# Sample states read a second time in turned layout in place of TensorE transposes, and two mask tiles moved to a short-lived pool

## The chip, the core and the metric

The kernel runs on one core of one Trainium2 chip. The metric is the device time of one launch in microseconds. The core has a matrix engine (TensorE, "PE" in the profile, with its weight loads listed as "PEld"), three elementwise engines (VectorE "DVE", ScalarE "ACT", GpSimd "POOL") and a queue engine (SyncE "SP") that here does nothing but issue DMA transfers. Each engine works through its own list of instructions strictly in order. An instruction that has to wait for another engine or for a transfer also holds everything behind it on its own engine.

## What is computed

One inference step of a two-layer decoder, for a prompt of 1024 tokens and for 8 samples of 8 tokens each. Layer 0 is a Mamba-2 state-space (SSD) mixer, layer 1 is latent attention. Only layer 0 is touched here. Cut to what matters:

```python
def ssd_mixer(h, conv_buf, ssm_state, w_in, ...):
    proj = jnp.einsum('btd,de->bte', h, w_in)          # z | x, B, C | dt
    xbc = silu(causal_conv(xbc, conv_buf, conv_w, conv_b))
    dt = softplus(dt_raw + dt_bias); a_head = -exp(a_log)
    y, new_state = ssd_scan(xs, dt, a_head, bm, cm, ssm_state)
    y = (y + d_skip[:, None] * xs) * silu(z)           # then a group norm and w_out

def ssd_scan(x, dt, a_head, bm, cm, init_state):
    # per chunk of up to 128 tokens, causal inside the chunk:
    y_diag = einsum('bgrcls,bcsgrp->bclgrp', cb * decay, xdt)
    # the state that enters the chunk is read through C:
    y_off = einsum('bclgn,bcgrpn->bclgrp', cc, prev) * decay_in
    # and carried on: state = chunk_decay * state + B^T (x dt decay_end)
```

For the samples the incoming state is the input `state_ssm`, of shape (1, 8 samples, 32 heads, 64, 128). It is needed in two forms. To be read through C (`y_off`) the index n of size 128 is contracted, so n has to lie on the 128 partitions. To be decayed, updated and written out as `sample_state_ssm`, it is handled with (head, p) on the partitions, as it lies in memory.

## The kernel before, in words

Layer 0 works in 8 groups of 4 heads. For each group the kernel projects the inputs (TensorE, `proj_piece`, tile `pj`, line 89; gates `pz`, line 101), convolves them on VectorE, and then scans: 8 prompt chunks and one sample chunk (`ssd_chunks`) mixed with 4 state steps for the samples (`ssd_states`, one step per half of the samples and pair of heads, 32 steps in all). While one group is scanned, the next group's projection is fed in between, and for the last group the output projection (`poa`). In each product, operands are split into a rounded high part and a remainder (`split`: ScalarE casts the high part on line 130, VectorE subtracts for the low part on line 136), and three products of these parts make one full-precision product.

A state step before the change, lines 710 to 736:

1. SP loads a 256 KB piece of the state, `s0`, with (head, p) on partitions (line 714; the profile calls the tile `s`).
2. TensorE turns it by four 128x128 transposes against the identity into a PSUM tile `s0p` (line 717).
3. ScalarE and VectorE split `s0p` into `sh` and `sl`.
4. TensorE multiplies them with C (`pv`, line 726), ScalarE copies and VectorE adds the result into `yo` (lines 728 and 729).
5. GpSimd multiplies `s0` by the decay (line 730), TensorE makes the update `sn` (line 733), VectorE adds it (line 735), and SP writes the new state out (line 736).

`s0` has two buffers. The PSUM tag "tr", of two banks, is shared by these transposes and the transposes of the chunks.

Two mask tiles, `masku` (128x128) and `masks` (64x128), are loaded near the start of the launch into the pool `cs`, which lives as long as layer 0. GpSimd makes from them `negu` and `negs` (line 177), which the chunks add before the exponential (line 631). The masks themselves are used once more, as weights of the cumulative sum in `ssd_dt` (lines 410 and 411). The gate and dt weights of group 0, `zdh` and `zdl`, are loaded and split in `load_zdt` (lines 367 to 385) on GpSimd, in a pool named `zd` that closes as soon as `ssd_dt` is done.

The order of instructions on each engine is not written out by hand. A scheduler in the tile framework takes the instructions in a simulated order of readiness, under the dependencies, the buffers and a few `issue_after` marks, so that a local edit may also move the instructions around it.

Of the kernel before, what the change touches and what calls it, by code (L numbers as in the profile page):

```python
# [8 lines left out]
F32 = mybir.dt.float32  # L9
F32R = mybir.dt.float32r  # L10
AF = mybir.ActivationFunctionType
ALU = mybir.AluOpType
# [26 lines left out]
NEG = -1e30  # L39
# [43 lines left out]
PB = dict(PB1)  # L83
# [44 lines left out]
def split(k, hi, lo, src, eng=None, parts=0):  # L128
    nc = k.nc
    k.cast = nc.scalar.copy(hi, src)  # L130
    n = parts and hi.shape[1] // parts
    for a in range(parts):
        s = slice(a * n, a * n + n)
        (eng or nc.vector).tensor_tensor(lo[:, s], src[:, s], hi[:, s].bitcast(F32), op=ALU.subtract)
    if not parts:
        return (eng or nc.vector).tensor_tensor(lo, src, hi.bitcast(F32), op=ALU.subtract)  # L136
# [12 lines left out]

def ssd_tiles(k):  # L150
    cp, nc = k.cs, k.nc
    k.masku = cp.tile([128, 128], F32, name="masku")
    k.masks = cp.tile([64, 128], F32, name="masks")
    k.negu = cp.tile([128, 128], F32, name="negu")
    k.negs = cp.tile([64, 128], F32, name="negs")
    k.blkm = cp.tile([64, NB], F32, name="blkm")
    k.yssq = cp.tile([128, 9, G], F32, name="yssq")
    k.tok = cp.tile([128, 9, 4, H], F32, name="tok")
    k.decp = cp.tile([128, H, 8], F32, name="decp")
    k.decs = cp.tile([128, 16, 8], F32, name="decs")  # L160
    k.dtb = cp.tile([128, H], F32, name="dtb")
    k.dsk = cp.tile([128, H], F32, name="dsk")
    k.tok3 = cp.tile([96, 2, H], F32, name="tok3")
    k.blk3 = cp.tile([96, 4], F32, name="blk3")
    k.alog = cp.tile([128, H], F32, name="alog")


def ssd_consts(k):
    nc, I = k.nc, k.I
    nc.sync.dma_start(k.alog, I["ssd_a_log"][0].partition_broadcast(128))  # L170
    with k.tc.issue_after(k.cols[1][7].ins):
        nc.scalar.activation(k.alog, k.alog, AF.Exp)
    nc.sync.dma_start(k.masku, I["c_masku"])
    nc.sync.dma_start(k.masks, I["c_masks"])
    for neg, mask in ((k.negu, k.masku), (k.negs, k.masks)):
        with k.tc.issue_after(k.pow.ins):
            nc.gpsimd.tensor_scalar(neg, mask, -NEG, NEG, op0=ALU.mult, op1=ALU.add)
    nc.sync.dma_start(k.blkm, I["c_blkm"])
    for j in range(3):
        nc.sync.dma_start(k.blk3[32 * j : 32 * j + 32], I["c_blkm"][:32, :4])  # L180
    nc.gpsimd.memset(k.yssq, 1.0)
    nc.sync.dma_start(k.dtb, I["ssd_dt_bias"][0].partition_broadcast(128))
    nc.sync.dma_start(k.dsk, I["ssd_d"][0].partition_broadcast(128))
# [185 lines left out]
def load_zdt(k, pool):  # L369
    nc = k.nc  # L370
    w = k.I["ssd_w_in"][0].rearrange("(k p) e -> p k e", p=128)
    k.wzd = []
    k.dtr = pool.tile([128, 9, H], F32, name="dtr")
    nc.gpsimd.memset(k.dtr[64:, 8], 0.0)
    for j in range(2):
        ks = slice(4 * j, 4 * j + 4)
        hi = pool.tile([128, 4, 288], F32R, name=f"zdh{j}")
        lo = pool.tile([128, 4, 288], F32R, name=f"zdl{j}")
        raw = load_raw(pool, 4, 288, 1)
        nc.sync.dma_start(raw[:, :, 0:256], w[:, ks, 0:256])  # L380
        nc.sync.dma_start(raw[:, :, 256:288], w[:, ks, DIN + CONV :])
        nc.gpsimd.tensor_copy(hi, raw)
        for a in range(4):
            nc.gpsimd.tensor_tensor(lo[:, a], raw[:, a], hi[:, a].bitcast(F32), op=ALU.subtract)
        k.wzd += kslices((hi, lo), 4)
# [290 lines left out]
def ssd_states(k, gr, pools):  # L676
    nc, I = k.nc, k.I
    sp, psum = pools
    g = gr.g
    hs = slice(4 * g, 4 * g + 4)  # L680
    tag = f"{g}_8"
    B, C, X0, X1 = (gr.xc[q][1][:, j] for q in range(2) for j in range(2))
    for q in range(2):
        t = k.cblk[q]
        dh, dl = (bass.AP(t.tensor, t[:, 0, o:].offset, [list(t.ap[0]), [72, 4], [1, NT]]) for o in (0, 32))
        Cv = C[:, 32 * q : 32 * q + 32].rearrange("p (b t) -> p b t", t=NT)
        nc.scalar.copy(dh, Cv)
        nc.vector.tensor_tensor(dl, Cv, dh.bitcast(F32), op=ALU.subtract)
    yo = gr.yo = sp.tile([128, 256], F32, tag="yo", name=f"yo{g}", bufs=1)
    for q in range(2):  # L690
        p = psum.tile([128, 512], F32, tag="tr", name=f"x3p{tag}{q}", bufs=PB["tr"])
        xr = sp.tile([128, 4, 128], F32, tag="M", name=f"xr3{tag}{q}", bufs=3)[:, :3, :96]
        for j, src in enumerate((X0, X1, B)):
            nc.gpsimd.tensor_copy(xr[:, j].rearrange("p (r t) -> p r t", r=3),
                                  src[:, 32 * q : 32 * q + 32].unsqueeze(1).to_broadcast([128, 3, 32]))
            nc.tensor.transpose(p[:96, j * 128 : j * 128 + 128], xr[:, j], k.ident)
        xf = sp.tile([128, 256], F32, tag="fo", name=f"xf{tag}{q}", bufs=1)[:96]
        nc.vector.tensor_tensor(xf.rearrange("p (h q) -> p h q", q=64),
                                p[:96, :256].rearrange("p (h q) -> p h q", q=64),
                                k.tok3[:, q, hs].unsqueeze(2).to_broadcast([96, 4, 64]), op=ALU.mult)  # L700
        x3 = sp.tile([96, 256], F32R, tag="x3", name=f"x3{tag}{q}", bufs=1)
        nc.scalar.copy(x3, xf)
        nc.vector.tensor_tensor(x3[32:64], xf[32:64], x3[32:64].bitcast(F32), op=ALU.subtract)
        b3 = sp.tile([96, 128], F32R, tag="b3", name=f"b3{tag}{q}", bufs=1)
        nc.scalar.copy(b3, p[:96, 256:384])
        nc.vector.tensor_tensor(b3[64:96], p[64:96, 256:384], b3[64:96].bitcast(F32), op=ALU.subtract)
        bb = sp.tile([96, 4, 128], F32R, tag="bb", name=f"bb{tag}{q}", bufs=1)
        nc.gpsimd.tensor_tensor(bb, b3.bitcast(F32).unsqueeze(1).to_broadcast([96, 4, 128]),
                                k.blk3.unsqueeze(2).to_broadcast([96, 4, 128]), op=ALU.mult)
        bs = slice(4 * q, 4 * q + 4)  # L710
        for pr in range(2):
            h0 = 4 * g + 2 * pr
            s0 = sp.tile([128, 4, 128], F32, tag="s0", name=f"s0{tag}{q}{pr}", bufs=2)
            nc.sync.dma_start(s0, I["state_ssm"][0, bs, h0 : h0 + 2].rearrange("b h p n -> (h p) b n"))
            pt = psum.tile([128, 512], F32, tag="tr", name=f"s0p{tag}{pr}{q}", bufs=PB["tr"])
            for b in range(4):
                nc.tensor.transpose(pt[:, b * 128 : b * 128 + 128], s0[:, b], k.ident)
            sh = sp.tile([128, 512], F32R, tag="sh", name=f"sh{tag}{pr}{q}", bufs=1)
            sl_ = sp.tile([128, 512], F32R, tag="sl", name=f"sl{tag}{pr}{q}", bufs=1)
            split(k, sh, sl_, pt)  # L720
            pv = psum.tile([128, 512], F32, tag="cb", name=f"pv{tag}{q}{pr}", bufs=PB["cb"])
            for b in range(4):
                sb = slice(b * 128, b * 128 + 128)
                x = [(pv[:32, :128], k.cblk[q][:, b, :32], sl_[:, sb]), (pv[:64, :128], k.cblk[q][:, b], sh[:, sb])]
                for j, (a, u, v) in enumerate(x if b else x[::-1]):
                    nc.tensor.matmul(a, u, v, start=(b + j == 0), stop=(b == 3 and j == 1))
            yr = yo[32 * q : 32 * q + 32, 128 * pr : 128 * pr + 128]
            k.yoc = nc.scalar.copy(yr, pv[32:64, :128])
            nc.vector.tensor_tensor(yr, yr, pv[:32, :128], op=ALU.add)
            nc.gpsimd.tensor_tensor(s0, s0, k.decs[:, h0 // 2, bs].unsqueeze(2).to_broadcast([128, 4, 128]),  # L730
                                    op=ALU.mult)
            pt = psum.tile([128, 512], F32, tag="st", name=f"sn{tag}{pr}{q}", bufs=PB["st"])
            nc.tensor.matmul(pt, x3[:, pr * 128 : pr * 128 + 128], bb.rearrange("p b n -> p (b n)"),
                             start=True, stop=True)
            nc.vector.tensor_tensor(s0, s0, pt.rearrange("p (b n) -> p b n", b=4), op=ALU.add)
            nc.sync.dma_start(k.O["s_ssm"][0, bs, h0 : h0 + 2].rearrange("b h p n -> (h p) b n"), s0)
            yield
# [1388 lines left out]
```

## Time and profile before

| what | value |
|---|---|
| runs of the kernel before | 1915.88, 1918.3 and 1923.65 us; median 1918.3 |
| span of the profiled execution, first to last instruction | 1915.0 us |
| TensorE busy | 1887.4 us (99%) |
| VectorE, ScalarE, GpSimd busy | 1208.5, 1101.1 and 823.3 us |
| DMA | 212.51 MB, mean 111 GB/s |
| layer 0 | from the start to about 922 us, its group scans from about 118 us |

The profile of the one execution shows its span and not a separate launch time; its span is 0.9 us under the fastest and 3.3 us under the median of the three runs. A line of a group reads: source line, engine, operation, output tile and input tiles, shapes and count, then busy time and the mean duration of one, then the idle time just ahead of them and what ended it. A matmul's recorded duration reaches past the start of the next one, since they are pipelined; how long a matmul holds the engine is the distance from its start to the start of the next.

### The profile page before, as it was taken

How to read it: one execution, taken by the hardware profiler on the slowest of the kernel's cores; microseconds unless marked ns; L12 is line 12 of the kernel's file. 1: busy time of each engine (PE TensorE's matmuls, PEld its weight loads, DVE VectorE, ACT ScalarE, POOL GpSimd, SP SyncE). 2: the span in 40 equal slices, each digit the busy share in tenths (PEclk: the TensorE clock that was granted, in tenths of full speed). 3: DMA queues.
4: the chain of work that ended last, by engine and by line, in shares of the span. 5: the costliest groups of instructions: out<-in, count | busy, mean ns of one | idle time of the engine just before them, and what ended most of it. 6: DMA issues, size and time to landing. Idle time of an engine off the chain costs nothing.

```text
span 1915.0 us, 33672 instructions
## 1 busy us (share of the span) xinstructions
PE 1887.4 (99%) x12023; PEld 1728.1 (90%) x12023; DVE 1208.5 (63%) x2500; ACT 1101.1 (57%) x2528; POOL 823.3 (43%) x1116
## 2 busy tenths in 40 slices
PE   8999999999999999999999999999999999999998
PEld 7999999999999999888788998898888887888887
DVE  5557676757676767765534214566887878666665
ACT  6467666767666666732214323436777777755552
POOL 2447555555655555453004322103443434764551
PEclk9999999999999999999999999999999999999999
DMA  5223323332323232644424662233111112664451
GB/s 165 54 79 91 94 83 94 88 106 83 101 84 99 85 99 78 212 158 175 166 110 133 209 226 75 69 110 95 47 52 41 53 41 58 228 204 142 146 170 37
DMA packets 183967, 212.51 MB, mean 111 GB/s; under 512 B 19148, under 2 KB 147928, under 8 KB 182776
## 3 DMA queue, kind: packets, MB, share of 16 engines
q1 hardware_dynamic: 177304, 185.32, 31.1%
q0 software_dynamic: 6416, 24.91, 3.8%
q8 instruction: 95, 1.56, 0.3%
q14 instruction: 72, 0.59, 0.1%
q10 hardware_dynamic: 80, 0.13, 0.0%
HBM read 151.76 MB, written 58.52 MB: 110 GB/s over the span
## 4 chain that ended last, share of the span: by engine, by line
PE 90%; DMA 3%; DVE 3%; ACT 3%; issue 1%; POOL 0%; SPq 0%; POOLq 0%; DVEq 0%; ACTq 0%
PE pj L89 24%; PE pz L101 8%; PE pq L101 6%; PE pob L101 5%; PE p L101 5%; PE poa L101 4%; PE py L640 3%; PE sc L89 3%; PE o L89 2%; PE sc L1402 2%; PE o L1465 2%; PE o L1467 2%; PE st L1434 2%; PE st L1435 2%; PE st L1436 2%; PE o L1466 2%
## 5 line engine op out<-in xcount | busy, mean ns | idle before, releaser
L89 PE MATMUL pj<-xl,wih 128*128 128x384 f32 (+1 forms) x768 | 255.4, 333 | 0.0
L89 PE MATMUL pj<-xh,wih 128*128 128x384 f32 (+1 forms) x768 | 252.9, 333 | 1.2 <-ACT xh L276 0.8
L89 PE MATMUL pj<-xh,wil 128*128 128x384 f32 (+1 forms) x768 | 252.9, 329 | 0.0
L1448 POOL TENSOR_TENSOR tl<-P,th 128x384 fp32r<-128x384 f32 (+1 forms) x96 | 90.6, 944 | 232.3 <-ACT P L1446 186.6
L528 DVE SCALAR_TENSOR_TENSOR acc<-raw,vec,acc 128x1112 f32<-128x1112 f32 x96 | 141.6, 1476 | 15.3 <-ACT acc L524 14.4
L89 PEld LDWEIGHTS pj<-xh,wih 128*128 128x128 f32 x768 | 143.8, 188 | 2.6 <-ACT xh L276 1.4
L89 PEld LDWEIGHTS pj<-xl,wih 128*128 128x128 f32 x768 | 144.5, 188 | 1.0
L89 PEld LDWEIGHTS pj<-xh,wil 128*128 128x128 f32 x768 | 144.5, 188 | 0.5
L101 PE MATMUL pz<-wih,xh 128*128 128x256 f32 x504 | 143.3, 288 | 1.4 <-ACT z L569 1.4
L101 PE MATMUL pz<-wil,xh 128*128 128x256 f32 (+1 forms) x504 | 139.8, 283 | 0.0
L1445 ACT ACTIVATE th<-st 128x512 fp32r<-128x512 f32 x192 | 94.6, 493 | 66.6 <-PE st L1441 50.9
L101 PE MATMUL pz<-wih,xl 128*128 128x256 f32 x448 | 128.5, 287 | 0.0
L1733 POOL TENSOR_TENSOR kvl<-pgr,kvh 128x256 fp32r<-128x256 f32 x128 | 97.8, 791 | 70.6 <-ACT kvh L1731 70.3
L635 ACT ACTIVATE M<-M,tok 128x128 f32<-128x128 f32 (+1 forms) x288 | 90.4, 386 | 51.4 <-DVE M L631 51.2
L136 DVE TENSOR_TENSOR wil<-wraw,wih 128x512 fp32r<-128x512 f32 x88 | 74.4, 851 | 38.2 <-ACT wih L130 31.7
L101 PEld LDWEIGHTS pz<-wih,xh 128*128 128x128 f32 x504 | 95.9, 190 | 2.3 <-ACT z L569 1.8
L1446 ACT ACTIVATE P<-st 128x512 f32<-128x512 f32 x192 | 93.5, 487 | 0.0
L101 PEld LDWEIGHTS pz<-wil,xh 128*128 128x128 f32 (+1 forms) x504 | 92.8, 184 | 0.1
L101 PE MATMUL p<-w,oh 128*128 128x512 f32 (+3 forms) x304 | 88.8, 386 | 0.6 <-DVE h L1983 0.6
L616 POOL TENSOR_TENSOR xdd<-xsT,tok 128x256 f32<-128x256 f32 x64 | 50.0, 781 | 86.4 <-ACT xsT L602 83.3
L101 PEld LDWEIGHTS pz<-wih,xl 128*128 128x128 f32 x448 | 85.4, 191 | 0.7
L1448 DVE TENSOR_TENSOR tl<-P,th 128x512 fp32r<-128x512 f32 x96 | 72.1, 752 | 18.9 <-ACT P L1446 18.7
(830 smaller groups left out, 6212.5 us busy)
## 6 DMA issues: line engine op xcount, KB each, us to landing
wraw<-in_ssd_w_in SPq DMA_DIRECT2D x92, 256.0 KB
M<-acs_d SPq DMA_DIRECT2D x64, 256.0 KB
s<-in_state_ssm SPq DMA_DIRECT2D x32, 256.0 KB
y_d<-y SPq DMA_DIRECT2D x64, 128.0 KB
out_s_ssm<-s SPq DMA_DIRECT2D x32, 256.0 KB
q_d<-qt SPq DMA_DIRECT2D x32, 192.0 KB
qp<-q_d SPq DMA_DIRECT2D x8, 768.0 KB
wraw<-in_ssd_w_out SPq DMA_DIRECT2D x10, 512.0 KB
```

The costliest lines, as they stand in the source:

```text
L89: nc.tensor.matmul(out, a, b, start=(i == 0), stop=(i == n - 1))
L101: nc.tensor.matmul(o, a, b, start=(j == 0), stop=(j == len(ops) - 1))
L136: return (eng or nc.vector).tensor_tensor(lo, src, hi.bitcast(F32), op=ALU.subtract)
L528: last = nc.vector.scalar_tensor_tensor(acc, raw[:, j : j + n], k.convw[j][:, blk : blk + 1], acc, op0=ALU.mult, op1=ALU.add)
L616: nc.gpsimd.tensor_tensor(v3(xdd), v3(xsT), hb(2), op=ALU.mult)
L635: nc.scalar.activation(M[:m, h, :m], M[:m, h, :m], AF.Exp, bias=tk[:, 0, 4 * g + h : 4 * g + h + 1])
L640: nc.tensor.matmul(py[:m, h * 64 : h * 64 + 64], M[:m, h, :m], xsT[:m, h * 64 : h * 64 + 64], start=True, stop=True)
L1402: nc.tensor.matmul(ps[:, :n], qh[:96, 128 * i : 128 * i + 128], kh[:96, 512 * c : 512 * c + n], start=True, stop=True)
L1445: nc.scalar.activation(th[:, :n], ps[:, :n], AF.Exp, scale=SCALE)
L1446: nc.scalar.activation(P[:, :n], ps[:, :n], AF.Exp, scale=SCALE)
L1448: eng.tensor_tensor(tl[:, :n], P[:, :n], th[:, :n].bitcast(F32), op=ALU.subtract)
L1733: nc.gpsimd.tensor_tensor(rl[:, j], raw[:, j], rh[:, j].bitcast(F32), op=ALU.subtract)
```

## The change

The state is given to the launch a second time as an input `c_turned`, laid out by numpy so that n comes first. Each of its 32 pieces of 256 KB is loaded by SP into a tile `s0t` of the same tag as `s0`, which now has three buffers, and is split from there, in SBUF. The four transposes of a step and their PSUM tile are gone. `s0` is still loaded for the decay and the update. The two masks are allocated in the pool `zd` and loaded in `load_zdt`, and the two instructions that make `negu` and `negs` stand there without the mark that had placed them after the last power instruction of the input norm. Lines behind the edits have other numbers in the changed kernel: 717 has no counterpart, 714 is 715 there, the new load is on 713, 726 is 724, 733 is 731, 736 is 734, 321 is 314.

```diff
 def ssd_tiles(k):
     cp, nc = k.cs, k.nc
-    k.masku = cp.tile([128, 128], F32, name="masku")
-    k.masks = cp.tile([64, 128], F32, name="masks")
...
 def ssd_consts(k):
-    nc.sync.dma_start(k.masku, I["c_masku"])
-    nc.sync.dma_start(k.masks, I["c_masks"])
-    for neg, mask in ((k.negu, k.masku), (k.negs, k.masks)):
-        with k.tc.issue_after(k.pow.ins):
-            nc.gpsimd.tensor_scalar(neg, mask, -NEG, NEG, op0=ALU.mult, op1=ALU.add)
...
 def load_zdt(k, pool):
+    k.masku = pool.tile([128, 128], F32, name="masku")
+    k.masks = pool.tile([64, 128], F32, name="masks")
+    nc.sync.dma_start(k.masku, k.I["c_masku"])
+    nc.sync.dma_start(k.masks, k.I["c_masks"])
+    for neg, mask in ((k.negu, k.masku), (k.negs, k.masks)):
+        nc.gpsimd.tensor_scalar(neg, mask, -NEG, NEG, op0=ALU.mult, op1=ALU.add)
...
 def ssd_states(k, gr, pools):
-            s0 = sp.tile([128, 4, 128], F32, tag="s0", name=f"s0{tag}{q}{pr}", bufs=2)
+            s0t = sp.tile([128, 4, 128], F32, tag="s0", name=f"s0t{tag}{q}{pr}", bufs=3).rearrange("p b n -> p (b n)")
+            nc.sync.dma_start(s0t, I["c_turned"][h0 // 2, q])
+            s0 = sp.tile([128, 4, 128], F32, tag="s0", name=f"s0{tag}{q}{pr}", bufs=3)
             nc.sync.dma_start(s0, I["state_ssm"][0, bs, h0 : h0 + 2].rearrange("b h p n -> (h p) b n"))
-            pt = psum.tile([128, 512], F32, tag="tr", name=f"s0p{tag}{pr}{q}", bufs=PB["tr"])
-            for b in range(4):
-                nc.tensor.transpose(pt[:, b * 128 : b * 128 + 128], s0[:, b], k.ident)
...
-            split(k, sh, sl_, pt)
+            split(k, sh, sl_, s0t)
...
 def kernel(**inputs):
+    st = given["state_ssm"][0].reshape(2, 4, 16, 128, 128).transpose(2, 0, 4, 1, 3)
+    given["c_turned"] = np.ascontiguousarray(st).reshape(16, 2, 128, 512)
```

The scheduler sets the order anew. What follows are three places of it.

**TensorE, a state step in the middle of layer 0** (`s0p` are the transposes, `sn` the state update, `pv` the product with C, `pj` the next group's projection). Before:

```order
L89 MATMUL pj<-xh,wil 128x320
L89 MATMUL pj<-xh,wih 128x320
L89 MATMUL pj<-xl,wih 128x320
L89 MATMUL pj<-xh,wil 128x320
L717 MATMUL s0p_810_5484<-ident,s_801_5482 128x128 x4
L733 MATMUL sn_810_5505<-bb_80_5183,x_80_5177 128x512
L89 MATMUL pj<-xh,wih 128x384
```

With the change:

```order
L89 MATMUL pj<-xl,wih 128x320
L89 MATMUL pj<-xh,wil 128x320
L724 MATMUL pv_801_5451<-sh_810_5447,cblk_1134 64x128
L724 MATMUL pv_801_5451<-sl_810_5448,cblk_1134 32x128 x2
L724 MATMUL pv_801_5451<-sh_810_5447,cblk_1134 64x128
L724 MATMUL pv_801_5451<-sl_810_5448,cblk_1134 32x128
L724 MATMUL pv_801_5451<-sh_810_5447,cblk_1134 64x128
L724 MATMUL pv_801_5451<-sl_810_5448,cblk_1134 32x128
L724 MATMUL pv_801_5451<-sh_810_5447,cblk_1134 64x128
L731 MATMUL sn_810_5463<-bb_80_5147,x_80_5141 128x512
L89 MATMUL pj<-xh,wih 128x384
```

The transposes are gone and the step's `pv` products have moved up to just ahead of the update.

**SP, the end of the state steps of a group** (`M` are decay rows for the chunks, `wraw` the next group's weights, `y_d` results of the chunks). Before:

```order
L630 DMA M_6_7371<-acs_d 128x512
L665 DMA y_d<-y_3_6948 128x256
L630 DMA M_7_7535<-acs_d 128x512
L665 DMA y_d<-y_4_7034 128x256
L321 DMA wraw<-in_ssd_w_in 128x4x128 x2
L736 DMA out_s_ssm<-s_810_7131 128x4x128
```

With the change:

```order
L664 DMA y_d<-y_3_6894 128x256
L629 DMA M_6_7314<-acs_d 128x512
L629 DMA M_7_7475<-acs_d 128x512
L664 DMA y_d<-y_4_6980 128x256
L713 DMA s0t_800_7749<-in_c_turned 128x512
L314 DMA wraw<-in_ssd_w_in 128x4x128 x2
L734 DMA out_s_ssm<-s_810_7079 128x4x128
L715 DMA s_800_7751<-in_state_ssm 128x4x128
```

A load of the turned state now stands ahead of two weight loads.

**GpSimd, early in the launch** (`zdh` and `zdl` are the split gate weights of group 0, `wil` the low half of a projection weight, `raw` the input of a convolution). Before:

```order
L382 CAST zdh_790<-wraw 128x1152
L136 TENSOR_TENSOR wil<-wraw,wih 128x512
L384 TENSOR_TENSOR zdl_791<-wraw,zdh_790 128x288 x4
L507 MEMSET raw_603 128x3
L518 COPY raw_603<-convT 128x8x3
```

With the change:

```order
L371 TENSOR_SCALAR negs<-masks 64x128
L521 COPY ct_105<-raw_257 128x24
L520 COPY ct_105<-raw_285 128x3
L521 COPY ct_105<-raw_285 128x24
L136 TENSOR_TENSOR wil<-wraw,wih 128x512
L381 CAST zdh_790<-wraw 128x1152
L506 MEMSET raw_597 128x3
L517 COPY raw_597<-convT 128x8x3
L383 TENSOR_TENSOR zdl_791<-wraw,zdh_790 128x288 x4
```

The weight remainder `wil` and the preparation of a convolution input now stand ahead of the first gate split. On SP the first gate weights stand behind the two mask loads and one projection weight load, where before they stood ahead of that load.

## The prediction

> **What bounds the kernel now.** I read the page's first lines and its chain first, then the busy times by stretch, then what TensorE waited for in layer 0.
>
> ```profile
> span 1915.0 us, 33672 instructions
> PE 1887.4 (99%) x12023; PEld 1728.1 (90%) x12023; DVE 1208.5 (63%) x2500; ACT 1101.1 (57%) x2528; POOL 823.3 (43%) x1116
> q1 hardware_dynamic: 177304, 185.32, 31.1%
> PE 90%; DMA 3%; DVE 3%; ACT 3%; issue 1%; POOL 0%; SPq 0%; POOLq 0%; DVEq 0%; ACTq 0%
> ```
>
> TensorE is busy for 99% of the span and carries 90% of the chain. So an edit pays only if TensorE's stream gets shorter without new holes in it. The stretch table (span of the stretch, then busy PE, PEld, DVE, ACT, POOL, the granted clock, DMA share, GB/s) shows a group in the middle of layer 0 and all that follows the layer's last scan:
>
> ```profile
> 300.00:400.00 100.00, 99.64 (x740) 98.10 (x738) 68.59 (x109) 67.23 (x166) 52.73 (x83) 1.00 0.31 90
> 895.00:1915.00 1020.00, 1003.96 (x5777) 878.82 (x5777) 617.93 (x1526) 537.70 (x1163) 361.71 (x417) 1.00 0.36 117
> ```
>
> In the group TensorE idles 0.36 us in 100, at full clock, while VectorE and ScalarE have some 31 us of idle time and the DMA engines two thirds. TensorE's waits between 100 and 895 us, longest first and then the one that belongs to a state step:
>
> ```profile
> PE pz L101 <- ACT z L569: 1.4, 2, 0.7
> PE cb L628 <- DVE yo L729: 1.1, 3, 0.4
> PE trp L597 <- DVE yla L136: 1.0, 1, 1.0
> PE pv L726 <- DVE sl L136: 0.2, 1, 0.2
> ```
>
> They are small, and none is a wait for a weight load or a state load. The stage is a stream of matmuls back to back, and whatever leaves the stream is time saved.
>
> **What the transposes cost.** There are 8 groups x 4 steps x 4 = 128 of them. Their recorded duration overstates them, so I take the distance between starts.
>
> ```profile
> 307.08 0.34 PE L89 MATMUL pj<-xh,wih 128*128 128x384 f32 x1
> 307.25 0.60 PE L717 MATMUL s0p<-ident,s 128*128 128x128 f32 x4
> 307.60 0.36 PE L89 MATMUL st<-xddl,BTh 128*128 128x256 f32 x1
> 307.81 0.28 PE L89 MATMUL st<-xddh,BTl 128*128 128x256 f32 x1
> 307.93 1.00 PE L640 MATMUL py<-xsT,M 128*128 128x64 f32 x8
> ```
>
> Four transposes start at 307.25, the next matmul at 307.60. That matmul then holds the engine 0.21 us, where its equal at 307.81 needs 0.12, so the change of kind costs another 0.09. From 307.25 to 307.81 are 0.56 us, less 0.12 for the `st` itself, 0.44 for four: 0.11 us each, 128 x 0.11 = 14.1 us. This is the value I take. The near end leaves the 0.09 in the stream, because some other transpose may stand there instead: 0.35 / 4 x 128 = 11.2 us. The far end is the union of their recorded durations in this table of groups (busy us, then mean ns of one, then the idle time ahead):
>
> ```profile
> L717 PE MATMUL s0p<-ident,s 128*128 128x128 f32 x128 | 20.5, 272 | 0.0
> L130 ACT CAST sh<-s0p 128x512 fp32r<-128x512 f32 x32 | 18.6, 582 | 1.6 <-PE s0p L717 1.6
> L136 DVE TENSOR_TENSOR sl<-s0p,sh 128x512 fp32r<-128x512 f32 x32 | 21.8, 683 | 1.4 <-ACT sh L130 1.3
> L130 ACT CAST wih<-wraw 128x512 fp32r<-128x512 f32 x77 | 46.8, 615 | 37.4 <-PE pj L89 23.6 <-DMA wraw<-in_ssd_w_in 13.7
> L136 DVE TENSOR_TENSOR wil<-wraw,wih 128x512 fp32r<-128x512 f32 x77 | 65.5, 856 | 32.3 <-ACT wih L130 28.3 <-PE pj L89 3.5
> L730 POOL TENSOR_TENSOR s<-s,decs 128x512 f32<-128x512 f32 x32 | 35.4, 1106 | 18.2 <-PE s0p L717 18.2
> ```
>
> 20.5 us, reached only if each also delays its neighbour beyond what the rows above show.
>
> **The split from SBUF.** The same cast and subtraction, on weights in SBUF, are `wih` and `wil` in the table. ScalarE goes from 582 to about 615 ns, 32 x 33 ns = 1.1 us; VectorE from 683 to about 856, 32 x 173 ns = 5.5 us. I cost both at nothing: over 32 steps in some 755 us they meet the 31 us of idle time per 100 quoted above. Without that cover they cost 6.6 us. GpSimd's decay on line 730 loses its 18.2 us of waiting for transposes, on an engine nobody waits for here, so I count no gain.
>
> The Trainium skill, on its page "SBUF — State Buffer", section "Who interferes with whom", speaks against this part: a VectorE instruction with two SBUF inputs contends with a GpSimd instruction that reads SBUF, and the later one waits for the whole of the other. The rows agree in direction, 683 ns with an input in PSUM against a mean of 856 with both in SBUF. By that rule a halving could lose a whole GpSimd operation such as line 730's 1.1 us, at most 32 x 1.1 = 35 us on VectorE, which is still less than its idle time.
>
> **Transfers and SP.** 32 loads of 256 KB are 8.4 MB. Queue q1 needed 31.1% of 16 engines' span for 185.32 MB, so these need 8.4 / 185.32 x 31.1% x 1915 = 27 us of all 16 engines, spread over 755: the busy share rises by under 0.04 from 0.31. SP needs 0.38 us for each issue, 12 us in all:
>
> ```profile
> L714 SPq DMA_DIRECT2D s<-in_state_ssm x32: 372/383/447, 119.5 to 834.8; - x32
> SPq L714 <- DMA out_s_ssm<-s: 42.7, 23, 3.7
> 400.27 0.39 SPq L321 DMA_DIRECT2D wraw<-in_ssd_w_in  x1
> 405.02 0.62 ACT L130 CAST wih<-wraw 128x512 fp32r<-128x512 f32 x1 [2.65 <-DMA wraw<-in_ssd_w_in]
> ```
>
> More serious is what an SP wait holds up. Behind a turned load stand weight loads. The row of SP's waits says that state loads already waited 42.7 us, in 23 pieces of up to 3.7, for a buffer to be written out, and no TensorE wait came of it. The tightest weight load I found is that at 400.27, whose cast at 405.02 had ScalarE waiting 2.65 us; even there TensorE did not wait. I take 0. The turned load itself has time: a step comes every 24 us (98 us a group, four steps). The third buffer lets it in while the old state is still being updated.
>
> **The masks.** Their use as weights and the use of `negu` come late:
>
> ```profile
> L410 PE MATMUL dpa<-dta,masku x2: 379/431/483, 108.6 to 108.9; 128*128 128x256 f32 x2
> L631 DVE TENSOR_TENSOR M<-M,negu x64: 673/754/1711, 123.5 to 854.1; 128x512 f32<-128x512 f32 x64
> ```
>
> At 108.6 and 123.5 us both will long be there. What can be late are the gate weights, whose load moves behind the masks on SP and whose split moves behind `wil` and a convolution's `raw` on GpSimd:
>
> ```profile
> 49.31 1.15 POOL L382 CAST zdh<-wraw 128x1152 fp32r<-128x1152 f32 x1
> 52.09 2.19 POOL L136 TENSOR_TENSOR wil<-wraw,wih 128x512 fp32r<-128x512 f32 x1 [1.63 <-ACT wih L130]
> 54.24 6.78 POOL L384 TENSOR_TENSOR zdl<-wraw,zdh 128x288 fp32r<-128x288 f32 x4
> 61.01 1.26 POOL L518 COPY raw<-convT 128x24 f32<-128x24 f32 x1
> 66.83 6.78 POOL L384 TENSOR_TENSOR zdl<-wraw,zdh 128x288 fp32r<-128x288 f32 x4
> 73.07 0.38 PE L101 MATMUL pz<-zdh,xh 128*128 128x288 f32 x1
> 75.93 0.29 PE L101 MATMUL pz<-zdh,xh 128*128 128x288 f32 x1
> ```
>
> New order: `wil` ends about 54.3 as before, then the cast (1.15), then `raw` (1.3), then the first `zdl` from 56.8 instead of 54.24. The second half shares the load buffer and shifts likewise, ending at 66.83 + 6.78 + 2.6 = 76.2. TensorE starts on these weights at 73.07 and reaches the last of the eight slices at 75.93: a hole of 0.3 us, which I take. It is 0 if `wil` is quicker, and 2 us if the load or `raw` also comes late.
>
> **Sum.** -14.1 + 0.3 = -13.8 us on 1915.0, so 1901.2 for a profiled span. The runs' median lies 3.3 us above that span; with the same distance I predict 1904. After layer 0 I expect nothing, since the orders fall into step there.
>
> **Rivals.**
>
> *More than its own time* (0.12). With the transposes gone the products stand closer together, and the far end holds: 1918.3 - 20.5 = 1898. For it: pieces of one or two transposes stand between other products. Against it: 0.11 fits both a run of four and its successor.
>
> *The full recorded time* (0.03). If a transpose really kept the stream for the 272 ns of its row, 34.8 us would go: 1884. Against it: four of them record 0.60 us, and the next matmul starts 0.35 after the first. The Trainium skill gives about 275 ns for a transpose in a kernel's context, on "TensorE: Matmul & The Clock Gate", section "Part 4: PE-mode transpose". The duration in the trace agrees; the distance between starts does not support it as a price.
>
> *The saved time comes back as waits* (0.17). The split's 6.6 us uncovered, plus 2 us at the start, leave -14.1 + 8.6 = -5.5: 1913. It needs ScalarE or VectorE to be the next limit where casts feed TensorE. Against it: 0.2 us of TensorE waiting for `sl` in the whole stage. For it: TensorE has no slack, and a new order may place a cast too late in any group.
>
> *SP holds up the weights* (0.05). A turned load waits on SP for the previous halving, the two weight loads behind it start late, and TensorE runs dry. It costs nothing up to the slack, and turns the change slower once a step loses over 14.1 / 32 = 0.44 us. At 0.75 us, 24.0 us in all, it gives 1918.3 + 10 = 1928. For it: the 4.75 us from issue to cast at 400.27. Against it: the old waits of up to 3.7 us cost nothing.
>
> **How the numbers follow.** My forecast has 0.63, with its own range of 1899 to 1909 from 11.2 to 17 us saved, give or take a run's noise. The range of 1896 to 1912 takes in the first rival and about half of the third. About 0.5%, 9.6 us, is what a measurement can tell from no change. Faster by more: forecast and the first two rivals, 0.78. Within it: the third, 0.17. Slower: the fourth, 0.05.
>
> **What would show it.** Right: no `s0p` in the trace, TensorE 99% busy, layer 0 shorter by about 1.7 us per group, `sl` at about 860 ns, the rest unchanged in length. Wrong: TensorE waits for `wih`, `wil`, `sl` or `zdl` of over a microsecond in a group, or SP waiting on line 713 with weight loads behind it and ScalarE waiting for `wraw`.

## The result, and the profile after

The changed kernel is slower. Its median is 1929.75 us (5 runs, 1927.48 to 1931.97), that of the kernel before in the same session 1915.88 us (5 runs, 1914.28 to 1923.65). The ratio is 1.0064, with a 95% interval of 1.0048 to 1.0079, so some 12 us were lost where 14 were forecast as gained. The profiled span grew from 1915.0 to 1925.9 us, by 10.9 us.

From the page of the changed kernel, its span, the engines' busy times, the shares of the chain that ended last, and one of the costliest groups:

```profile
span 1925.9 us, 33490 instructions
PE 1880.3 (98%) x11895; PEld 1717.6 (89%) x11895; DVE 1203.2 (62%) x2500; ACT 1100.8 (57%) x2528; POOL 833.9 (43%) x1116
PE 70%; DMA 5%; DVE 4%; POOL 4%; ACT 4%; issue 2%; SPq 0%; POOLq 0%; DVEq 0%; ACTq 0%
L728 POOL TENSOR_TENSOR s<-s,decs 128x512 f32<-128x512 f32 x32 | 35.3, 1104 | 115.5 <-DMA s<-in_state_ssm 91.9
```

TensorE has exactly 128 matmuls fewer (12023 to 11895) and is busy for 7 us less, as wanted. But the chain, 90% TensorE before, is now 70% TensorE, and GpSimd has 4% of it where it had none. The last row says why: ahead of its 32 decays GpSimd, which before waited 18.2 us for the transposes, now stands idle for 115.5 us, and 91.9 of these are ended by the state's load.

Where the time went, stage by stage. The table of stretches of the kernel before, first from the first product with the masks as weights (`dpa`) to the last of layer 0's output projection (`poa`), then to the end:

```profile
108.60:922.00 813.40, 807.72 (x5735) 774.50 (x5736) 554.43 (x921) 516.46 (x1280) 434.51 (x640) 1.00 0.36 110
922.00:1915.00 993.00, 976.96 (x5642) 857.44 (x5640) 601.58 (x1500) 527.05 (x1149) 354.83 (x415) 1.00 0.35 113
```

The same stretches of the changed kernel (columns: length, then busy PE, PEld, DVE, ACT, POOL, clock, DMA share, GB/s):

```profile
108.00:933.70 825.70, 802.30 (x5608) 766.29 (x5608) 550.15 (x921) 515.51 (x1279) 449.57 (x640) 0.99 0.40 118
933.70:1925.90 992.20, 974.63 (x5642) 854.82 (x5640) 602.22 (x1500) 527.61 (x1149) 354.82 (x415) 1.00 0.36 114
```

The whole loss lies in the scans of layer 0: 825.7 - 813.4 = 12.3 us. TensorE's idle time in that stage is length minus busy time: 813.40 - 807.72 = 5.7 us before, 825.70 - 802.30 = 23.4 us after. So 17.7 us of idle time came in, and only 5.4 us of busy time went out with the 128 transposes.

Part of the busy time is a lower clock. The kernel before ran this stage at a granted clock of 1.00 throughout. The changed kernel has three pieces of 3.4 us at 0.50 (the third value from the end of each row), where some 5 us of full-clock work are lost:

```profile
148.50:151.90 3.40, 3.40 (x19) 3.40 (x18) 2.37 (x3) 1.45 (x5) 2.90 (x6) 0.50 0.11 39
206.50:209.90 3.40, 3.40 (x18) 3.40 (x18) 2.28 (x5) 1.90 (x4) 0.73 (x1) 0.50 0.37 104
797.00:800.40 3.40, 3.40 (x18) 3.40 (x17) 2.39 (x6) 0.26 (x1) 3.32 (x6) 0.50 0.69 236
```

The first begins 1.3 us after the end of TensorE's longest wait in the stage, 2.97 us. That the waits bring the pieces about was not tested.

Here is what TensorE waited for between 100 and 895 us in the changed kernel (total, times, longest):

```profile
PE st L89 <- POOL xddl L136: 10.1, 9, 3.0
PE st L89 <- ACT xddh L130: 5.1, 6, 1.3
PE py L89 <- POOL Sl L136: 3.1, 7, 1.2
```

None of these stood in the list before. They are the chunks' own products: `xddl` and `Sl` are remainders that GpSimd makes for the prompt chunks, and `xddh` is the high part that ScalarE casts from GpSimd's `xdd`. None is a piece of a sample state. The longest such wait, on GpSimd, SyncE and TensorE of the changed kernel (start us, duration us, then in brackets the idle time ahead and what ended it):

```profile
136.57 0.68 POOL L521 COPY ct<-raw 128x24 f32<-128x24 f32 x1
144.96 1.04 POOL L728 TENSOR_TENSOR s<-s,decs 128x512 f32<-128x512 f32 x1 [7.72 <-DMA s<-in_state_ssm]
145.96 1.17 POOL L136 TENSOR_TENSOR xddl<-xdd,xddh 128x256 fp32r<-128x256 f32 x1
```

```profile
137.81 0.40 SPq L734 DMA_DIRECT2D out_s_ssm<-s  x1
141.80 0.37 SPq L715 DMA_DIRECT2D s<-in_state_ssm  x1
```

```profile
143.91 0.30 PE L89 MATMUL pj<-xl,wih 128*128 128x320 f32 x1
147.19 0.39 PE L89 MATMUL st<-xddl,BTh 128*128 128x256 f32 x1 [2.97 <-POOL xddl L136]
172.86 0.39 PE L731 MATMUL sn<-bb,x 96*128 96x512 f32 x1
```

GpSimd is done with `ct` at 137.25, and the next instruction on its list is the decay of a state whose load SyncE only issues at 141.80. GpSimd stands idle for 7.72 us, until the load has landed, 3.2 us after its issue. Some 4.5 us of that pass before the load is even issued: the trace has SyncE's state loads wait 60.5 us in 27 pieces for old states to be written out. Behind the decay stands `xddl`, and TensorE waits 2.97 us for it. The decayed state is wanted by VectorE's addition of `sn`, and `sn` is made at 172.86, 27 us later. So GpSimd did this work long before it was wanted, and made the chunk late by it.

In the kernel before, the same step looks like this, on SyncE, TensorE and GpSimd:

```profile
135.93 0.37 SPq L714 DMA_DIRECT2D s<-in_state_ssm  x1
```

```profile
160.70 0.60 PE L717 MATMUL s0p<-ident,s 128*128 128x128 f32 x4
```

```profile
163.53 1.04 POOL L730 TENSOR_TENSOR s<-s,decs 128x512 f32<-128x512 f32 x1
```

The decay overwrites `s0`, so it has to stand behind the transposes that read `s0`, and these come 25 us after the load was issued. Over all 32 steps the median from the load's issue to the decay is 42.2 us before and 3.1 us after, and the median from the decay's end to the product `sn` is 2.4 us before and 38.6 us after. The transposes had kept the decay late, and so had covered the load. With them gone nothing kept the decay from standing right behind its load, and the scheduler put it there.

### The profile page after: what moved, and what is told of

It reads as the page before. It is cut to its first block, busy times and chain, and to the rows that moved or that the text cites. A ratio compares the mean times of both kernels' runs of the same rounds, so it can differ in the third digit from the quotient of the medians.

```text
span 1925.9 us, 33490 instructions
## 1 busy us (share of the span) xinstructions
PE 1880.3 (98%) x11895; PEld 1717.6 (89%) x11895; DVE 1203.2 (62%) x2500; ACT 1100.8 (57%) x2528; POOL 833.9 (43%) x1116
## 4 chain that ended last, share of the span: by engine, by line
PE 70%; DMA 5%; DVE 4%; POOL 4%; ACT 4%; issue 2%; SPq 0%; POOLq 0%; DVEq 0%; ACTq 0%
PE pj L89 14%; PE pq L101 6%; PE pob L101 5%; PE p L101 5%; PE poa L101 4%; PE pz L101 3%; PE sc L89 3%; PE o L89 2%; PE sc L1400 2%; PE o L1463 2%; PE o L1465 2%; PE st L1432 2%; PE st L1433 2%; PE st L1434 2%; PE o L1464 2%
## 5 line engine op out<-in xcount | busy, mean ns | idle before, releaser
L136 DVE TENSOR_TENSOR wil<-wraw,wih 128x512 fp32r<-128x512 f32 x88 | 64.3, 738 | 41.1 <-ACT wih L130 39.1
L662 DVE TENSOR_TENSOR y<-y,z 128x256 f32<-128x256 f32 (+1 forms) x72 | 51.2, 710 | 57.7 <-POOL y L659 57.7
L728 POOL TENSOR_TENSOR s<-s,decs 128x512 f32<-128x512 f32 x32 | 35.3, 1104 | 115.5 <-DMA s<-in_state_ssm 91.9
```

The costliest lines, as they stand in the source:

```text
L662: nc.vector.tensor_tensor(y[:m], y[:m], z, op=ALU.mult)
```

## The experiments

The expectations call the split of the state "halving", and name the theories that they set against each other by letters.

**The decay put late again.** The change as it is, with the decay issued behind the product `xD` of the chunk that is under way:

```diff
-            nc.gpsimd.tensor_tensor(v3(xD), v3(xsT), ...)
+            k.xdi = nc.gpsimd.tensor_tensor(v3(xD), v3(xsT), ...)
...
-            nc.gpsimd.tensor_tensor(s0, s0, k.decs...)
+            with k.tc.issue_after(k.xdi.ins):
+                nc.gpsimd.tensor_tensor(s0, s0, k.decs...)
```

> The changed kernel, with one mark more: GpSimd's decay of the old state is queued behind the xD product of the chunk that the step follows, so that it stands one state step later in GpSimd's list; nothing else is edited. Theory A (the transposes used to hold the decay back; without them it stands right behind the load of the old state, GpSimd waits there about 3 us after each issue, and the chunk work behind it reaches TensorE late): GpSimd's wait for the state load falls from 91.9 us to under 10, TensorE's waits from 100 to 895 us from 23.9 back to about 6, and the time to about 1930 - 26 = 1904 us. Rival B (the 32 more loads on SP's queue delay the others) and rival C (the masks in the pool that closes early) and rival D (halving from SBUF): the time stays at 1926 to 1932, since loads, masks and halving are untouched.

Measured: 1911.15 us (6 runs), a ratio of 0.9963 (0.9950 to 0.9975) to the kernel before, so 18.6 us under the change. The group of the decays, and the stage, in this kernel:

```profile
L729 POOL TENSOR_TENSOR s<-s,decs 128x512 f32<-128x512 f32 x32 | 36.4, 1137 | 1.5 <-DMA s<-in_state_ssm 1.5
```

```profile
108.50:914.50 806.00, 797.87 (x5608) 764.40 (x5608) 561.80 (x920) 510.74 (x1277) 458.85 (x640) 1.00 0.41 121
```

GpSimd's idle time ahead of the decays falls from 115.5 to 1.5 us (the median from a decay's end to `sn` is 7.6 us here), TensorE's idle time in the stage from 23.4 to 8.1 us, and the stage from 825.7 to 806.0. TensorE's waits for `xddh` are gone from its list with most of those for `xddl`. The decay's place explains the sign. It does not explain everything: the stage is 7.4 us shorter than before, where 14.1 were forecast.

**The masks alone.** The kernel before, with only the masks' part of the change:

> The kernel before with the masks' part of the change alone: masks in the pool that closes early, states and transposes as before. Theory A and rivals B and D: within 2 us of the kernel before (about 1916), since the decay, the loads and the halving are as before. Rival C: most of the 14 us of the change, 1926 or more.

Measured: 1921.26 us (12 runs), ratio 1.0017 (1.0008 to 1.0026), so some 3 us slower. That is far from the 1926 us of rival C. At the layer change, between 1015 and 1150 us, TensorE has a wait there that the kernel before does not show:

```profile
PE pj L89 <- DVE hl L270: 1.7, 1, 1.7
```

The forecast cost of the masks, 0.3 us, was for another place, the start of the gate products.

**A second copy that is still transposed.** The extra load of 256 KB is kept, but it brings the state as it lies in memory, and the four transposes read this copy. Everything else is as in the change; once with the decay where the schedule puts it, once tied as above.

```diff
-            nc.sync.dma_start(s0t, I["c_turned"][h0 // 2, q])
+            nc.sync.dma_start(s0t, I["state_ssm"][0, bs, h0 : h0 + 2]...)
...
+            for b in range(4):
+                nc.tensor.transpose(pt[:, b * 128 : b * 128 + 128], s0t[:, b], k.ident)
...
-            split(k, sh, sl_, s0t)
+            split(k, sh, sl_, pt)
```

> The changed kernel with the second load taken from the state as it lies, and TensorE's four transposes of each step kept, on that second copy; the halving reads PSUM as before. So the transposes are all there and only the tie between them and the decay is gone. Theory A: the waits are those of the changed kernel and the transposes come on top, 1930 + 14 = about 1944, and GpSimd waits some 90 us for state loads. Rival B: the same time, but with TensorE waiting for weights, decay rows or states and not for GpSimd. Rival D: 1916 to 1920, as the halving is that of before.

> The same as the run with the transposes kept on a second copy, with the decay queued behind the chunk's xD product as in the first run. Loads: 8.4 MB more than before, on the same queue. Theory A: back to the kernel before, 1914 to 1920. Rival B: as slow as without the mark, about 1944, since every load is still there. Rival D: no difference between the two runs.

Measured: 1930.57 us (ratio 1.0064, 1.0049 to 1.0079) free, 1934.72 us (1.0088, 1.0073 to 1.0103) tied. GpSimd's wait for the state's load is 48.9 us free and 1.9 us tied, but the tied one gains nothing. Both forecasts of theory A, 1944 and 1914 to 1920, were missed. In these two kernels something else costs time, so the pair does not single out the decay. In the scans of the free one TensorE waits longest for `bb` (3.9 us), `ct` and `yo` (2.6 us each) and only 0.5 us for `xddl`; in the tied one for `yo` (3.4 us), `sl` and `bb` (1.7 us each). The pair raised the question whether the second load is dear by itself.

**The loads, in three ways.** First the loads alone, into a tile that nothing reads, on the kernel before with the masks moved; then the tied change, and the tied copy, with the two copies in buffers of their own (one and two, in place of three shared ones); and the untied change with these buffers.

```diff
-            s0t = sp.tile([128, 4, 128], F32, tag="s0", name=..., bufs=3)
+            s0t = sp.tile([128, 4, 128], F32, tag="s0t", name=..., bufs=1)
...
-            s0 = sp.tile([128, 4, 128], F32, tag="s0", name=..., bufs=3)
+            s0 = sp.tile([128, 4, 128], F32, tag="s0", name=..., bufs=2)
```

> The kernel before with the masks moved, and with the turned states loaded into a tile of their own that nothing reads (so the 32 extra transfers of 256 KB are there, and no order, wait or shared buffer of the change). Theory T (the traffic of the extra loads is what costs the tied copy its 13 us above the masks alone): near that kernel, 1931 us, 1926 to 1936. Theory Q (what costs it is that both loads turn in the same three buffers, so that a load stands on SyncE waiting for a store of 4 to 5 us, 23 to 27 times, and holds the loads behind it): near the masks alone, 1921 us, 1918 to 1925.

> The tied decay (GpSimd's decay behind the xD product), and the two copies in buffers of their own: one for the turned one, two for the state, as large together as the three. Theory Q: SyncE's waits for the store of the states (62.6 us, 27 times with three shared buffers) go, and part of the 8 us that the tied kernel still lacks comes back: 1904 us, 1899 to 1908. Theory T: the same transfers, the same time: 1911 us, 1908 to 1914.

> The tied copy with the transposes kept (1934.7 us), and the two copies in buffers of their own. Theory Q: falls to about the masks alone, 1922 us, 1918 to 1927. Theory T: stays at 1934 us, 1930 to 1938.

> The change with the two copies in buffers of their own and the decay where the schedule puts it. If GpSimd's wait for the state's load is what makes the change slower, the wait decides here too: if it stays near 92 us in 21 waits, 1920 us or more; if the other order of the loads lets the state land before GpSimd reaches the decay (waits under 20 us), 1905 to 1912 us.

Measured: loads alone 1939.94 us (ratio 1.0105, 1.0091 to 1.0120); tied change, buffers apart, 1911.19 us (0.9953, 0.9940 to 0.9966); tied copy, buffers apart, 1933.08 us (1.0079, 1.0063 to 1.0096); untied change, buffers apart, 1931.97 us (1.0074, 1.0061 to 1.0086).

The first was not the experiment it was meant to be. With no reader the scheduler issued the 32 loads in one bunch, as their issue row says (duration min/median/max in ns, first and last start in us), and the time was lost there:

```profile
L713 SPq DMA_DIRECT2D s0t<-in_c_turned x32: 327/328/459, 119.2 to 214.5; - x32
108.60:289.40 180.80, 164.40 (x1136) 160.10 (x1137) 110.65 (x183) 110.59 (x279) 85.75 (x139) 0.96 0.45 129
289.40:945.40 656.00, 651.52 (x4603) 621.14 (x4600) 442.03 (x738) 407.35 (x1005) 339.79 (x502) 1.00 0.38 114
```

The first two groups took 180.8 us, against 159.8 in the kernel before, and the other six 656.0 against 653.6 (with the masks alone they took 161.5 and 654.7):

```profile
108.60:268.40 159.80, 158.40 (x1136) 154.56 (x1137) 113.52 (x183) 108.08 (x277) 95.79 (x139) 1.00 0.32 94
268.40:922.00 653.60, 649.32 (x4602) 619.94 (x4600) 440.91 (x738) 408.38 (x1005) 338.71 (x502) 1.00 0.37 114
```

So a bunch of 32 loads costs some 20 us (TensorE idles for 16.4 of the 180.8 us, at a granted clock of 0.96), but it says nothing about loads that come one in 24 us. Buffers of their own bring nothing for the change or for the copy, so theory Q, that the shared buffers cost the time, falls. The untied change with its buffers apart keeps the wait and keeps the loss:

```profile
POOL s L728 <- DMA s<-in_state_ssm: 91.2, 22, 7.6
```

**The controls.** Two on the kernel before with the masks moved: the tie alone, and the extra loads, again without a reader but spread, each tied behind the state's own load. One on the tied change with buffers apart: the turned loads issued from ScalarE. And the change without any decay, which leaves out a part of the computation: its states come out undecayed.

```diff
+            with k.tc.issue_after(sld.ins):          # loads spread; sld is the state's own load
+                nc.sync.dma_start(s0t, I["c_turned"][h0 // 2, q])
...
-            nc.sync.dma_start(s0t, I["c_turned"][h0 // 2, q])
+            nc.scalar.dma_start(s0t, I["c_turned"][h0 // 2, q])   # turned loads from ScalarE
...
-            nc.gpsimd.tensor_tensor(s0, s0, k.decs...)             # no decay
```

> The kernel before with the masks moved, transposes and one load kept, and the decay tied behind the xD product as in the tied kernel. It is the control for the copies: if the tie costs nothing by itself (theory T), it stands with the masks alone, 1921 us, 1918 to 1924, and the 12 us of the tied copy are the second load's. If the tie costs them (the decay, held back, comes late for the state's update), 1930 us, 1926 to 1935.

> The kernel before with the masks moved, and the turned states loaded one by one, each directly behind its state's load on SyncE, into a tile that nothing reads; the loads on their own went in a bunch at 119 to 214 us, and cost 20 us there and nothing later. Theory T: 32 loads spread over the stage cost what the tied copy lost above the masks, 1931 us, 1927 to 1936. If a spread load costs nothing: 1921 us, 1918 to 1924.

> The tied decay with buffers apart (1911.2 us), its turned loads issued from ScalarE, so that no load stands behind them on SyncE; the traffic is the same. If what the tied kernel still lacks against the full 14 us is SyncE's order, 1905 us, 1901 to 1908. If it is the traffic, 1911 us. If ScalarE, waiting in its order for the turned tile to come free, holds its other work back, over 1914 us.

> The change without GpSimd's decay of the sample states, which is left out of the computation. It takes GpSimd's wait for the load away (91.9 us) and with it 35.3 us of its work. If the wait is the cause, and nothing else of the change, it must come to the tied kernel's time or a little under it: 1908 us, 1903 to 1912. If the cause is the second load or the masks alone, GpSimd has no part, and it stays near 1929 us, 1925 to 1932.

Measured: the tie alone 1922.08 us (ratio 1.0017, 1.0007 to 1.0027), which is the masks alone; the loads spread 1922.99 us (1.0024, 1.0015 to 1.0034), some 1 us more, which the intervals do not tell from none; turned loads from ScalarE 1910.33 us (0.9950, 0.9935 to 0.9966), as the tied change; no decay 1912.03 us (0.9956, 0.9941 to 0.9970), also as the tied change. The stage of the kernel without a decay:

```profile
109.90:915.30 805.40, 797.56 (x5608) 763.61 (x5608) 545.26 (x920) 512.50 (x1277) 415.35 (x608) 1.00 0.41 121
```

It is 805.4 us long, against 806.0 with the decay put late. Whether the decay is taken out or put late, the same 18 to 21 us come back. So the decay's work on GpSimd costs nothing that shows, and its early place behind the load is what cost the time. The loads spread are almost free, and moving the turned loads off SyncE brings the tied change nothing. Theory T, that the traffic costs 12 us, falls with the spread loads. What makes the transposed copies slow is then neither the tie, nor the loads, nor the shared buffers, each taken by itself; it stays open.

**The masks in place.** In the tied change the masks were no longer moved, but turned into `negu` and `negs` in their own tiles after the products that read them:

```diff
-    k.masku = pool.tile(...); k.masks = pool.tile(...)     # in load_zdt, with loads and GpSimd's two operations
+    k.masku = k.negu = cp.tile([128, 128], F32, name="negu")
+    k.masks = k.negs = cp.tile([64, 128], F32, name="negs")
...
+    for neg in (k.negu, k.negs):                           # in ssd_dt, behind the products dpa
+        nc.gpsimd.tensor_scalar(neg, neg, -NEG, NEG, op0=ALU.mult, op1=ALU.add)
```

> The tied kernel (ratio 0.9963 to before), its two masks not moved into the early pool: they are loaded where the kernel before has them, and turned into the additive masks in place once the two products that read them as masks are done, so that the room is the same. If what the tied kernel still lacks against the forecast (7 us) is for more than half the moved masks (measured alone at 3.8 us), 1907 us, 1904 to 1909, and a ratio of 0.993 to 0.995. If the masks' price was another thing of that kernel's order, 1911 us, 1909 to 1914, and 0.996 to 0.997.

Measured: 1910.76 us, ratio 0.9964 (0.9950 to 0.9977): the same as the tied change. In its trace the wait at the layer change is still there:

```profile
PE pj L89 <- DVE hl L272: 1.5, 1, 1.5
```

So the new place of the masks does not make this wait, since the wait remains without it. What these kernels share is two tiles fewer in the constants' pool. Whether that delays `hl`, and how, was not settled.

## Why the prediction was wrong

**The step that failed** is the sentence "GpSimd's decay on line 730 loses its 18.2 us of waiting for transposes, on an engine nobody waits for here, so I count no gain." Both halves were wrong. The decay did not lose a wait but exchanged 18.2 us for the transposes against 91.9 us for its load. And TensorE does wait for GpSimd, since `xddl` and `Sl` come from it on the same list. The waits of the kernel before gave no row for these two only because GpSimd had been on time. A short wait for GpSimd did stand in that list, though, just behind the first three rows, which the prediction shows:

```profile
PE ctp L536 <- POOL ct L522: 1.0, 1, 1.0
```

I read small waits as proof that nobody depends on the engine. The right question was what stands behind the decay on GpSimd's list. The prediction asked what the transposes cost and never what they held back: the write to `s0` behind their read. The order rows on record show TensorE and SyncE around a state step, and GpSimd only early in the launch. On GpSimd's list around a state step the decay's new place could have been seen.

The Trainium skill, on its page "PSUM — Partial Sum Buffer", section "Engine vs sequencer instructions", says that "ScalarE/VectorE/GpSimdE queues are strict FIFO". The trace agrees: `xddl` at 145.96 follows the decay that had kept GpSimd idle for 7.72 us.

**The transposes** were priced about right, as far as an estimate goes. I priced every matmul of the stage by the lower quartile, over fourteen of the kernels, of the distance to the next start among matmuls with neighbours of the same shapes. By that estimate the stream of the kernel before is 796.1 us long, that of the changed kernel 782.8 and that of the tied one 780.9, so 13 to 15 us shorter; 14.1 were forecast. It is rough: with the neighbours told apart by their tiles too, the tied kernel's stream is 14 us shorter but the changed one's only 3, since its waits then enter the prices. Neither "more than its own time" (20.5 us) nor "the full recorded time" (34.8 us) is borne out.

**The split from SBUF** cost TensorE nothing that shows: there is no wait for `sl` in the list above. Its rows in the changed kernel:

```profile
L130 ACT CAST sh<-s0t 128x512 fp32r<-128x512 f32 x32 | 19.7, 614 | 2.7 <-DMA s0t<-in_c_turned 2.6
L136 DVE TENSOR_TENSOR sl<-s0t,sh 128x512 fp32r<-128x512 f32 x32 | 25.5, 798 | 4.2 <-ACT sh L130 4.1
```

ScalarE's 614 ns is the forecast 615; VectorE's mean of 798 is below the forecast 856.

**Transfers and SP** were right at 0 or nearly: spread, the extra loads cost some 1 us, and issued from ScalarE they bring the same time. The rival "SP holds up the weights" (1928 us) was near the measured time in its number alone: a late load was the cause, but GpSimd waited for it, and no weight load came late: ScalarE's waits for the projection's `wraw` in the scans fell from 13.7 to 6.0 us. None of the waits that the prediction named as signs of being wrong reached TensorE; those that did had not been named.

**The masks** were mis-sized: 0.3 us forecast, some 3 us measured alone (1.5 to 5). The 0.3 us was expected at the gate products, where the changed kernel shows no hole. Where the 3 us lie is open. The wait at the layer change is in the changed kernel too (1.6 us), but its stretch behind the scans is no longer than before (992.20 against 993.00 us), so "After layer 0 I expect nothing" holds in the sum.

**What is still missing.** With the decay put late the kernel gains 6 or 7 us of the forecast 13.8. Against the tie alone (ratio 1.0017), which has the moved masks and the same tie but keeps the transposes, the tied change (0.9963) gains some 10 us. So the masks would account for some 3 us of what is missing, if the parts simply add up; the run with the masks in place does not show that they do, for it gains no more. The rest may be the loads' some 1 us and many short waits, as in the rival "the saved time comes back as waits" (1913 us): TensorE idles for 8.1 us of the tied kernel's stage, and for 5.7 before. Its clock has two pieces of 3.4 us at half there, at 184.9 and 778.8 us. TensorE's longest waits in the tied change, between 100 and 895 us:

```profile
PE py L89 <- ACT Sh L130: 1.9, 2, 1.7
PE poa L101 <- ACT M L634: 1.4, 1, 1.4
PE st L89 <- POOL xddl L136: 1.4, 2, 0.9
PE sn L732 <- POOL bb L707: 1.1, 2, 0.8
```

They come from ScalarE and GpSimd, not from the state's split or the start, which that rival had named.

## What to carry to other kernels

An instruction that is removed may have been holding another one back, through a buffer that it reads and the other writes. So for each read that goes, look up the next writer of the tile, ask where it will stand on its own engine's list, what it will wait for there, and what is queued behind it. Idle time on an engine that feeds the bottleneck is no proof that the bottleneck does not depend on it. And when work is wanted much later than it can start, say so in the order: here one tie turned a loss of 0.64% into a gain of about 0.4%.

## What the runs showed of the hardware

The subtraction of a split is steady with one input in PSUM and not with both in SBUF. Its durations, first before and then after (min/median/max in ns):

```profile
L136 DVE TENSOR_TENSOR sl<-s0p,sh x32: 677/681/692, 129.3 to 874.2; 128x512 fp32r<-128x512 f32 x32
```

```profile
L136 DVE TENSOR_TENSOR sl<-s0t,sh x32: 672/688/2027, 125.3 to 861.3; 128x512 fp32r<-128x512 f32 x32
```

The longest one, on VectorE and on GpSimd of the changed kernel:

```profile
133.53 2.03 DVE L136 TENSOR_TENSOR sl<-s0t,sh 128x512 fp32r<-128x512 f32 x1
```

```profile
133.09 1.22 POOL L707 TENSOR_TENSOR bb<-b,blk 96x512 fp32r<-96x512 f32 x1
134.27 0.74 POOL L136 TENSOR_TENSOR Sl<-S,Sh 128x256 fp32r<-128x256 f32 x1
```

It starts while GpSimd works on `bb`, and ends at 135.56, 0.55 us after GpSimd's next operation `Sl`: as if it had stood by for a part of their work. (Its own 0.69 from the end of `Sl`, 135.01, would make 135.70.) The rule quoted in the prediction from the Trainium skill ("SBUF — State Buffer", "Who interferes with whom") would make it wait for `bb`, which was under way. The trace agrees that it took 2.03 us in place of 0.69, but not in the length: `bb` ends at 134.31, and 0.69 from there would make 135.00. No run here tests it. GpSimd's subtraction grew too: `xddl` took 883 ns on average before and 1145 after.

```profile
L136 POOL TENSOR_TENSOR xddl<-xdd,xddh 128x256 fp32r<-128x256 f32 x64 | 56.5, 883 | 40.2 <-ACT xddh L130 36.4 <-PE cb L628 3.2 <-DVE BTl L136 0.5
```

```profile
L136 POOL TENSOR_TENSOR xddl<-xdd,xddh 128x256 fp32r<-128x256 f32 x64 | 73.3, 1145 | 27.6 <-ACT xddh L130 27.3 <-PE cb L627 0.3
```

That is 16.8 us more on GpSimd's list in the stage. In the two kernels without the wait, tied and without a decay, it is 996 ns, so part of it goes with the wait and part remains; it is a candidate for the short waits above, but nothing here shows it.
